# A blocked matmul with GELU: another home for one partial result, and another order for twelve loads

## Chip, cores, metric

One core of a Trainium2 chip. The time is that of one execution on the device in microseconds (us); lower is better. Unless a run says otherwise, times are medians of several executions. A profile is one further look at one execution, and its times are counted from that execution's first instruction.

## The reference

```python
m, k, n = 4096, 4096, 4096
a, b = randn(m, k), randn(k, n)           # float32
x = a @ b
out = 0.5 * x * (1 + tanh(sqrt(2 / pi) * (x + 0.044715 * x**3)))
```

## The kernel before

The kernel halves the matrices each way (A11, A12, ... B22) and computes blocks with seven products M1 to M7 instead of eight (a scheme of Strassen's kind), in 16-bit floats. There are 16 blocks. Block 0 must start before its data is there: the first half of its contraction (suffix _0) is done plainly, quadrant by quadrant, in 16 steps; the second half (suffix _1) with the seven products M3, M5, M7, M1, M4, M2, M6. A full product is 64 matmuls in four quarters; in block 0's second half only its last two quarters, 32 matmuls, are left. What the plain half gives for the output quarters is kept as partials C12 and C21 and added later.

TensorE accumulates in two chains of PSUM banks: X takes M5, M7, M1, M4 one on top of the other, Y takes M3, M2, M6. So a product may start on a bank only when the copy or result of the one before it has been read out. VectorE makes the sums of quadrants (aS, bS), transposes A (aT), and forms the results; ScalarE copies banks out (`keep`; such a copy is called a snapshot below) and does the GELU; GpSimd issues the loads.

```python
PRODUCTS = [                       # name, chain, sum of A, sum of B
    ("M3", "Y", "11", ("12", "22", 1)),
    ("M5", "X", ("11", "12", -1), "22"),
    ("M7", "X", ("12", "22", -1), ("21", "22", 1)),
    ("M1", "X", ("11", "22", -1), ("11", "22", -1)),
    ("M4", "X", "22", ("21", "11", 1)),
    ("M2", "Y", ("22", "21", -1), "11"),
    ("M6", "Y", ("21", "11", -1), ("11", "12", 1)),
]
# ... in plain(n): what becomes of a partial (i is one of RT = 4 row blocks)
            elif quad == "12":
                post[c, i] = keep("x7", acc, RT)
# ... in settle(gi, name, i), after the last matmul of a product on bank i
        if name == "M5":
            ...
                m5 = keep("m5", X, 2)
            y = new_y()                               # one of 5 output buffers
            tt(y, Y, m5, ALU.subtract)
            waiting.append((gi, i, 0, 1, y, y))
        elif name == "M7" and not end:
            post["x7", i] = keep("x7", X, RT)
        elif name == "M1":
            post["x1", i] = keep("x1", X, RT)
            later.append((gi, i))
        elif name == "M2":
            y = new_y()
            tt(y, post.pop(("x1", i)), Y, ALU.subtract)
            ...
        elif name == "M6":
            y = new_y()
            tt(y, Y, post.pop(("x7", i)), ALU.add)
            ...
# ... flush(): adds the partial of block 0 to a waiting result, then GELU and output
# ... the loads of block 0 by step: A, B load, T transpose; "+" weaves two loads evenly
        (8, "A11_1+B12_1+B22_1"),
        (9, "T22_0 A12_1+B21_1"),
        (14, "T11_1 A22_1 B11_1"),
        (16, "T12_1 A21_1"),
# ... the main loop
        for n, step in enumerate(steps):
            for fn, args in before.get(n, ()):        # loads and transposes
                fn(*args)
            if n + AHEAD < len(steps):                # AHEAD = 2
                gi, s, q = steps[n + AHEAD]
                if s >= 0:
                    make_sums(gi, s, q)
            if step[:2] != (0, 2):
                flush()
            combine()
            plain(n) if step[1] < 0 else multiply(*step)
            if step == (0, 2, QPH - 1):
                flush()
```

## Time and profile before

| | before |
|---|---|
| time, median of 3 | 1579.69 us (1579.39 to 1583.17) |
| span of the profiled execution | 1579.0 us |
| TensorE busy | 1566.6 us, 99% |
| VectorE busy over the whole span; in 74.2 to 122.4 us | 78%; 47.80 of 48.20 us |
| waits of TensorE in block 0's second half | 1.28, 0.38, 0.41, 1.80 and, entering the third quarter of block 1's M3, 0.28 us |

The kernel is bound by TensorE almost everywhere. The lines that carry this stand in the prediction. In rows in order of time, the first number is the start, the second the duration, and the bracket is the idle time of the engine before the row with what ended it.

### The profile page before, as it was taken

The numbers are of one execution on the slowest core, as the hardware profiler recorded it, in microseconds if no ns is written. First come the engines' busy times: TensorE is split into PE (matmuls) and PEld (weight loads), VectorE is DVE, ScalarE is ACT, GpSimd is POOL, SyncE is SP. The second block draws the span as 40 slices with busy tenths as digits, with TensorE's granted clock in tenths as the row PEclk, the third lists the DMA queues.
The fourth block names the chain that finished last, engine by engine and source line by source line (L and its number), as shares of the span: only waits on it lengthen the run. The fifth ranks groups of instructions, "written<-read, shape, count | busy, mean of one in ns | idle before, by whom it ended". The sixth has DMA issues, their size and how long they took to land. (4 is left out here: it accounts for less than half of the span.)

```text
span 1579.0 us, 19681 instructions
## 1 busy us (share of the span) xinstructions
PE 1566.6 (99%) x7246; PEld 709.1 (45%) x7246; DVE 1233.6 (78%) x1381; ACT 517.7 (33%) x710; POOL 537.6 (34%) x980
## 2 busy tenths in 40 slices
PE   9999999999999999999999999999999999999998
PEld 4444444444444444444444444444444444444443
DVE  1598888967787888895778788887687778988775
ACT  1026445311122545531111344542211145364111
POOL 7763442430234144341124413245011443314400
PEclk9999999999999999999999999999999999999999
DMA  9998784892957388586497837779468885748802
GB/s 179 197 223 175 123 171 74 159 168 43 197 104 153 92 133 160 107 174 120 83 162 117 186 72 141 148 112 186 77 121 146 134 160 94 149 105 134 160 28 82
DMA packets 225047, 211.13 MB, mean 134 GB/s; under 512 B 20144, under 2 KB 192176, under 8 KB 224944
## 3 DMA queue, kind: packets, MB, share of 16 engines
q0 software_dynamic: 187648, 142.67, 61.4%
q1 hardware_dynamic: 37296, 67.13, 11.8%
q8 instruction: 59, 0.97, 0.2%
q14 instruction: 44, 0.36, 0.1%
HBM read 285.22 MB, written 67.11 MB: 223 GB/s over the span
## 5 line engine op out<-in xcount | busy, mean ns | idle before, releaser
L331 PEld LDWEIGHTS <-aS 128*128 128x128 f16 x4960 | 485.3, 98 | 589.8 <-issue 2.8
L186 POOL DMA_DIRECT2D bR<-in_b_dram x832 | 447.6, 544 | 696.8 <-DVE bS L302 331.9
L302 DVE TENSOR_TENSOR aS<-aT 128x2048 f16<-128x2048 f16 (+1 forms) x312 | 376.3, 1212 | 150.2 <-PE accX L331 113.8
L331 PE MATMUL accX<-bS,aS 128*128 128x512 f16 x1984 | 431.5, 379 | 2.6 <-ACT x L395 1.8
L302 DVE TENSOR_TENSOR bS<-bR 128x2048 f16<-128x2048 f16 x310 | 376.2, 1218 | 69.0 <-PE accX L331 58.5
L331 PEld LDWEIGHTS <-aT 128*128 128x128 f16 x1984 | 194.1, 98 | 234.5 <-issue 0.6
L422 ACT ACTIVATE y<-y 128x512 f32<-128x512 f32 x192 | 118.2, 630 | 348.3 <-DVE y L431 348.2
L331 PE MATMUL accX<-bR,aS 128*128 128x512 f16 x992 | 216.7, 379 | 1.3 <-DVE aS L302 1.3
L331 PE MATMUL accY<-bS,aT 128*128 128x512 f16 x992 | 216.9, 379 | 0.3 <-DVE bS L302 0.3
L331 PE MATMUL accY<-bR,aS 128*128 128x512 f16 x992 | 216.7, 379 | 0.0
L331 PE MATMUL accX<-bS,aT 128*128 128x512 f16 x992 | 216.7, 379 | 0.0
L331 PE MATMUL accY<-bS,aS 128*128 128x512 f16 x992 | 216.7, 379 | 0.0
L186 POOL DMA_DIRECT2D stage<-in_a_dram x144 | 89.9, 631 | 252.7 <-DVE aT L161 178.7
L431 DVE TENSOR_TENSOR energy<-energy,square 128x1024 bf16<-128x1024 bf16 x240 | 164.5, 686 | 9.9 <-ACT square L207 5.7
L395 ACT COPY x<-accX 128x512 f32<-128x512 f32 x128 | 74.9, 585 | 227.1 <-PE accX L331 221.1
L207 ACT ACTIVATE square<-aT 128x1024 bf16<-128x1024 f16 x120 | 123.5, 1051 | 70.7 <-DVE energy L431 70.3
L207 ACT ACTIVATE square<-bR 128x1024 bf16<-128x1024 f16 x120 | 123.0, 1050 | 62.1 <-DVE energy L431 60.7
L161 DVE STREAM_TRANSPOSE aT<-stage 128x2048 uint32<-128x2048 uint32 (+1 forms) x37 | 74.6, 2018 | 48.1 <-DMA stage<-in_a_dram 42.0
L395 ACT COPY m<-accX 128x512 f32<-128x512 f32 x60 | 34.7, 579 | 219.5 <-PE accX L331 216.4
L422 ACT ACTIVATE y<-accX 128x512 f32<-128x512 f32 x64 | 38.2, 597 | 100.1 <-PE accX L331 99.9
L431 DVE TENSOR_TENSOR x<-accX,x 128x512 f32<-128x512 f32 x64 | 44.0, 691 | 21.8 <-ACT y L422 19.0
L431 DVE TENSOR_TENSOR y<-accY,m 128x512 f32<-128x512 f32 x60 | 39.9, 687 | 12.5 <-ACT m L395 12.4
(38 smaller groups left out, 343.0 us busy)
## 6 DMA issues: line engine op xcount, KB each, us to landing
bR<-in_b_dram POOLq DMA_DIRECT2D x832, 128.0 KB, 5.2
out_dram<-y SPq DMA_DIRECT2D x256, 256.0 KB, 5.6
stage<-in_a_dram POOLq DMA_DIRECT2D x112, 256.0 KB, 6.7
stage<-in_a_dram POOLq DMA_DIRECT2D x32, 128.0 KB, 5.1
row<-seen_d SPq DMA_DIRECT2D x2, 1.5 KB, 4.4
seen_d<-seen SPq DMA_DIRECT2D x1, 3.0 KB, 6.4
```

The lines of the kernel that those rows point to most:

```text
L161: nc.vector.transpose(dst[:, :, x, :], src[:, :, x, :])
L186: nc.gpsimd.dma_start(out=dst, in_=src)
L207: nc.scalar.activation(t[:, :], src, ACT.Square)
L302: nc.vector.tensor_tensor(out=x, in0=y, in1=z, op=ALU.add if o[2] > 0 else ALU.subtract)
L331: nc.tensor.matmul(acc[:, :], sa[:, j // 2, i * P : (i + 1) * P, j % 2], sb[:, j, :], start=start and j == 0, stop=stop and j == 3, skip_g ...
L395: nc.scalar.copy(out=t[:, :], in_=src[:, :])
L422: nc.scalar.activation(y[:, :], src[:, :], ACT.Gelu_apprx_tanh)
L431: nc.vector.tensor_tensor(out=o[:, :], in0=x[:, :], in1=y[:, :], op=op)
```

## The change

It aims at two of the waits. Partial C12 lay in the buffers of M7's snapshot, so the snapshot had to wait until C12 was added; it moves to those of M1's snapshot, which are needed one product later. And A12_1, for which M5 waits, is woven with only half of B21_1 (every second of its tiles, "a"), the other half ("b") following.

```diff
             elif quad == "12":
-                post[c, i] = keep("x7", acc, RT)
+                post[c, i] = keep("x1", acc, RT)
@@ the loads
-        (9, "T22_0 A12_1+B21_1"),
+        (9, "T22_0 A12_1+B21_1a B21_1b"),
@@ their reading: a suffix a or b picks a half
-                args = [(x[0], (0, x[1:3], int(x[4]), h)) for x in what.split("+")]
+                args = [
+                    (x[0], (0, x[1:3], int(x[4]), "ab".index(x[5]) if x[5:] else h))
+                    for x in what.split("+")
+                ]
```

## The prediction

> **What bounds the kernel now.** I read the page first, then the table of waits for TensorE, then the matmuls in order of time, then VectorE in order of time over the same stretch, and last the loads one by one.
>
> ```profile
> PE 1566.6 (99%) x7246; PEld 709.1 (45%) x7246; DVE 1233.6 (78%) x1381; ACT 517.7 (33%) x710; POOL 537.6 (34%) x980
> ...
> 129.70:1573.30 1443.60, 1443.60 (x6688) 654.34 (x6687) 1157.56 (x1293) 493.18 (x670) 445.29 (x811) 1.00 0.69 127
> 74.20:122.40 48.20, 44.34 (x204) 19.73 (x203) 47.80 (x55) 13.94 (x24) 33.31 (x61) 1.00 1.25 219
> ```
>
> The first line is the page's busy times; the other two are rows of the table by stretches (length, then busy time and count of PE, PEld, DVE, ACT, POOL, then granted clock, DMA share, GB/s). TensorE bounds the kernel: from 129.7 us to the end it is never idle. Nothing can be won there, and both parts of the change act earlier, in the first of the blocks. In 74.2 to 122.4 us it is VectorE that is full: 47.80 of 48.20 us.
>
> ```profile
> PE accX L331 <- ACT x L395: 1.8, 1, 1.8
> PE accX L331 <- DVE aS L302: 1.7, 2, 1.3
> ...
> 69.42 7.07 PE L331 MATMUL accY<-bS,aT 128*128 128x512 f16 x32
> 77.77 7.08 PE L331 MATMUL accX<-bR,aS 128*128 128x512 f16 x32 [1.28 <-DVE aS L302]
> 84.69 0.59 PE L331 MATMUL accX<-bS,aS 128*128 128x512 f16 x2
> 85.66 1.47 PE L331 MATMUL accX<-bS,aS 128*128 128x512 f16 x6 [0.38 <-DVE aS L302]
> 87.54 5.34 PE L331 MATMUL accX<-bS,aS 128*128 128x512 f16 x24 [0.41 <-ACT m L395]
> 94.68 7.07 PE L331 MATMUL accX<-bS,aS 128*128 128x512 f16 x32 [1.80 <-ACT x L395]
> 101.58 7.07 PE L331 MATMUL accX<-bS,aT 128*128 128x512 f16 x32
> ...
> 129.66 7.07 PE L331 MATMUL accY<-bS,aT 128*128 128x512 f16 x32 [0.28 <-DVE bS L302]
> ```
>
> The rows are the products of block 0's second half: M3 (69.42), M5 (77.77), M7 (84.69), M1 (94.68), M4, M2, M6, then M3 of block 1 at 122.30, whose third quarter starts at 129.66. An undisturbed product of 32 matmuls takes 101.58 - 94.68 = 6.90 us, 0.216 us each. From 69.42 to 129.66 there are 256 matmuls, 55.27 us, in 60.24 us: TensorE loses **4.97 us** here, in five places: about 1.44 before M5, 0.54 and 0.58 inside M7, 1.96 before M1, 0.45 at 129.66 (start to start, so a little more than the bracketed idle times). That is the ceiling for this change, 0.31% of the time.
>
> ```profile
> 69.62 0.69 DVE L431 TENSOR_TENSOR x<-x,accY 128x512 f32<-128x512 f32 x1 [0.67 <-PE accY L362]
> 74.14 2.31 DVE L161 STREAM_TRANSPOSE aT<-stage 128x2048 uint32<-128x2048 uint32 x1 [3.83 <-DMA stage<-in_a_dram]
> 76.49 2.36 DVE L302 TENSOR_TENSOR aS<-aT 128x2048 f16<-128x2048 f16 x2
> ...
> 93.27 2.49 DVE L431 TENSOR_TENSOR y<-y,x 128x512 f32<-128x512 f32 x4
> ...
> 118.16 2.50 DVE L431 TENSOR_TENSOR y<-y,c 128x512 f32<-128x512 f32 x4
> ...
> 125.05 0.69 DVE L431 TENSOR_TENSOR y<-accY,x 128x512 f32<-128x512 f32 x1 [2.66 <-DMA out_dram<-y]
> ...
> 128.39 1.22 DVE L302 TENSOR_TENSOR bS<-bR 128x2048 f16<-128x2048 f16 x1
> ```
>
> VectorE stands idle for 3.83 us until the last piece of A12_1 lands, turns it (74.14), makes M5's aS (76.49; M5 has waited for it), and then runs in order without a gap of note to 122.4. The row at 93.27 adds partial C12 to M5's results. ScalarE's copy of M7 goes into the same four buffers, so it waits for this row, and M1, which accumulates in M7's bank, waits for the copy: the 1.80 us. The row at 128.39 is the sum that M3 of block 1 waits for at 129.66. So the wait at 129.66 is the end of a VectorE chain that began at 74.14.
>
> **What the Trainium skill says.** "TensorE: Matmul & The Clock Gate", back-to-back issue gap: 512 columns at full clock, some 216 ns apart; the trace has 216 ns (6.90 us / 32), so a product cannot go faster. "VectorE: DVE Perf Modes", the perf-mode tier table and the errata section: a 16-bit tensor_tensor of 2048 elements 1224 ns, an fp32 one of 512 elements 691 ns; the trace has 1.22 us and 0.69 us, so these rows do not shrink. "Perfetto Trace Analysis", Tensor Engine Instruction: Vector and Scalar engines are strict FIFO; the trace agrees (the row at 93.27 stands behind M1's sums at 88.73 to 93.3 though its operands were older). "DMA: Bandwidth & Descriptors", issuing engines are not separate DMA queues: all DMAs share 16 engines and interleave; here the 12 loads concerned land in the order of issue, at 196 to 200 GB/s over that stretch.
>
> **Part 1, the C12 buffers.** No instruction is added or taken away: ScalarE's four copies, VectorE's adds are the same rows with other buffers. Removed: M7's copies no longer wait for the row at 93.27; the build of the changed kernel shows them waiting for TensorE alone. M7's first bank is then copied in 0.28 + 0.59 us after its last matmul, some 2.6 us before M7 ends, so M1 starts unhindered. Added: M1's copies must wait for C12's add. M1's first bank ends at about 90.3 + 4.3 = 94.6 us by then, the add ends before 93.5: no wait. By itself this pulls TensorE forward by 1.96 us at M1, but VectorE's rows do not move, so M3 of block 1 still waits for the row at 128.39. **Worth alone: about 0.**
>
> **Part 2, the loads.** The 12 loads are 4 of A12_1 (256 KB) and 8 of B21_1 (128 KB), 16 units of 128 KB. They land from 64.3 (58.74 + 5.6) to 74.7 us (67.32 + 7.4), issue time plus time to landing read row by row; the load before ends at about 63.65, so a unit takes (74.7 - 63.65) / 16 = 0.69 us. The order was b A b b A b b A b b A b: the fourth A is behind 15 units and lands at 66.67 + 7.4 = 74.07. The changed kernel issues A b A b A b A b b b b b: 11 units, 63.65 + 7.6 = 71.25, that is **2.8 us earlier**. VectorE is free from 70.3, so the transpose starts at 71.35 instead of 74.14. The last B21_1 piece still lands at 74.7 and is needed at 78.8 - 2.8 = 76.0. A22_1's second half lands at 74.97 + 5.1 = 80.1, is needed at 83.64 - 2.8 = 80.8: near, but in time.
>
> Now the sum, both parts together. VectorE, dense from the transpose on, runs 2.8 us earlier throughout. M5 starts at 76.33 (loss gone), M7 at 83.2 (its sums are ready at 82.1 and 82.8), M1 at 90.2, M4 97.1, M2 104.0, M6 110.9, M3 of block 1 at 117.8, its third quarter could start at 124.7. The sum it needs is ready at 129.6 - 2.8 = 126.8: a wait of **about 2.1 us**, in place of 0.3. Before that row VectorE waits for an output buffer: 118.16 + 0.69, gelu 0.63, landing some 5.5 us later, 125.05; all of it is set off by VectorE, so it moves by 2.8 as well if the landing takes as long. So TensorE recovers about 4.97 - 2.1 = 2.8 us: VectorE's shift, not the sum of the waits. From there on TensorE is dense, and the end moves by as much: 1579.69 - 2.8 = 1576.9; I say **1577.0**.
>
> **Rivals.** (a) The waits add up: all five go and nothing replaces them, -5.0 us, 1574.7. For it: 1.96 + 1.44 are named by the table of waits, and the two parts of the change aim exactly at them. Against it: VectorE's 47.80 of 48.20 us; for 5 us its chain would have to start before A12_1 can land. (b) The A12 pieces land no earlier, or A22_1 or B21_1 become the new wait, because the DMA engines are full either way: then VectorE's start moves by under 1 us and the time is 1579 to 1579.7. For it: only 0.7 us of reserve at A22_1, and POOL lets only eight loads be open at a time. Against it: the order within a full queue is exactly what the change alters, and the queue lands in order. (c) The output landing at 125.05 does not move along, because it competes with the loads of block 1 (landings there take 5.3 to 7.6 us, loads up to 9.7): it could eat 1 us or give 1: 1576 to 1578.
>
> **Range and chances.** The chain reading with a shift of 2.8 +- 0.8 us has some 7 in 10, (b) 1 in 10, between the two readings and towards (a) the rest. Runs of the kernel before spread from 1579.39 to 1583.17, so a median may be off by half a us: 1575.4 to 1579.0. 2% would be 31.6 us, six times the ceiling, and nothing that is added could cost as much: faster 0.005, within 2% 0.99, slower 0.005.
>
> **What would show it.** Right: the transpose at about 71.3; M5 at 76.4 with no wait; no wait of M1 for ScalarE; VectorE still without gaps to about 119.6; a wait for bS of about 2 us at the third quarter of block 1's M3, which starts near 126.9; nothing after. Wrong: if that wait stays below 0.5 us and the gain is over 4 us, VectorE was no bound; if VectorE waits for A22_1 at 80, rival (b); if the transpose comes early and the row after 125 does not, rival (c).

## The result, and the profile after

The changed kernel took 1578.82 us (1577.87 to 1579.90, 6 runs), the kernel before, of the same rounds, 1580.76 us (1579.39 to 1583.17, 6 runs). The ratio of the times is 0.9988, interval 0.9975 to 1.0001. That is 1.9 us less, inside the range, but less than the 2.8 us forecast; and no difference that the interval alone proves.

First view: the waits of TensorE in the changed kernel (total, times, longest, in us).

```profile
PE accY L331 <- DVE y L431: 1.8, 1, 1.8
PE accX L343 <- DVE table L583: 1.4, 1, 1.4
PE accY L331 <- DVE bS L302: 0.5, 1, 0.5
PE accY L362 <- DMA bR<-in_b_dram: 0.5, 1, 0.5
```

Both waits that the change aimed at are gone. The first line is new, and the prediction did not have it. Second view: TensorE's rows in order of time, from M3 in block 0 on.

```profile
70.27 7.07 PE L331 MATMUL accY<-bS,aT 128*128 128x512 f16 x32
77.18 7.07 PE L331 MATMUL accX<-bR,aS 128*128 128x512 f16 x32
84.08 14.05 PE L331 MATMUL accX<-bS,aS 128*128 128x512 f16 x64
97.97 7.07 PE L331 MATMUL accX<-bS,aT 128*128 128x512 f16 x32
104.88 7.07 PE L331 MATMUL accY<-bR,aS 128*128 128x512 f16 x32
113.72 7.07 PE L331 MATMUL accY<-bS,aS 128*128 128x512 f16 x32 [1.77 <-DVE y L431]
120.62 7.07 PE L331 MATMUL accY<-bS,aT 128*128 128x512 f16 x32
128.23 7.07 PE L331 MATMUL accY<-bS,aT 128*128 128x512 f16 x32 [0.54 <-DVE bS L302]
```

M3 to M2 run through without a wait. Then M6 (113.72) stands 1.77 us, and the third quarter of block 1's M3 (128.23) 0.54 us. Third view: VectorE's rows in order of time that the argument needs.

```profile
72.09 2.31 DVE L161 STREAM_TRANSPOSE aT<-stage 128x2048 uint32<-128x2048 uint32 x1 [0.93 <-DMA stage<-in_a_dram]
...
81.99 1.25 DVE L161 STREAM_TRANSPOSE aT<-stage 128x1024 uint32<-128x1024 uint32 x1 [0.44 <-DMA stage<-in_a_dram]
...
112.99 2.48 DVE L431 TENSOR_TENSOR y<-x,accY 128x512 f32<-128x512 f32 x4
...
116.51 2.49 DVE L431 TENSOR_TENSOR y<-y,c 128x512 f32<-128x512 f32 x4
...
123.45 0.69 DVE L431 TENSOR_TENSOR y<-accY,x 128x512 f32<-128x512 f32 x1 [2.71 <-DMA out_dram<-y]
```

The row at 112.99 is what M6 waits for: M2's results, read out of the Y banks on which M6 accumulates. They could be formed from about 109 us on (M2's first bank is full 20 matmuls after 104.88), but the four rows of sums for M6 stand ahead of them on VectorE.

The start-up is not the change's doing, but it moves the numbers. M3 starts at 70.27 us here and at 69.42 before. The 46 warm-up matmuls on zeros ended later here (the plain part started at 14.37 against 13.07 us), a difference that a later wait for a load (0.49 instead of 0.94 us) took partly back. A repeat of the same kernel (`after_again`, below) started M3 at 69.32 us, a repeat of the kernel before at 69.55. So three measures are used, each a difference between starts of rows; the first two leave the start-up out:

- **load lead**: VectorE's transpose of A11_1 to its transpose of A12_1. Small is early.
- **chain**: the transpose of A12_1 to the third quarter of block 1's M3 on TensorE. Where that row is merged with the half before it, 6.905 us (32 matmuls) are added to M3's start.
- **stretch**: block 0's M3 to that third quarter. It also holds how far the loads are behind TensorE: stretch = load lead + chain - the time from A11_1's transpose to M3, which was 6.81 us before and after, but between 5.33 and 6.81 us in the 14 profiles.

| | load lead | chain | stretch |
|---|---|---|---|
| before | 11.53 | 55.52 | 60.24 |
| after | 8.63 | 56.14 | 57.96 |

The stretch fell by 2.28 us; 0.85 us of it is missing from the span because of the later start, and the output at the very end landed about 0.5 us sooner: 1579.0 - 2.28 + 0.85 - 0.5 = 1577.1, the span measured. The load lead fell by 2.9 (2.8 forecast). The chain grew by 0.62, where the forecast had it constant.

### The profile page after: what moved, and what is told of

The parts are those of the page before. It is cut to its first block, busy times and chain, and to the rows that moved or that the text cites. A ratio compares the mean times of both kernels' runs of the same rounds, so it can differ in the third digit from the quotient of the medians.

```text
span 1577.1 us, 19678 instructions
## 1 busy us (share of the span) xinstructions
PE 1567.7 (99%) x7246; PEld 709.6 (45%) x7246; DVE 1233.7 (78%) x1381; ACT 518.0 (33%) x710; POOL 537.7 (34%) x980
```

## The experiments

Twelve runs. **Theory D** (the prediction's): VectorE, filled in order from the transpose of A12_1 on, sets the end of the stretch, so a wait removed downstream comes back as another. **Theory A**: each removed wait is a gain of its own.

### Each part alone, and both kernels again

The edits: `c12_only` has only the first hunk of the diff, `loads_only` only the others; `after_again` and `before_again` are the two kernels unchanged.

> Part 1 alone (C12 in M1's buffers, loads as before). Measure: the stretch from the first matmul of M3 in block 0 to the third quarter of M3 in block 1, 60.24 us before and 57.96 us after, which leaves out the start-up. Theory D (VectorE's dense chain sets the stretch): the 1.80 us before M1 goes, a wait of about 1.8 us before M6 for VectorE's y rows appears, stretch 60.2 +- 0.3, time ratio 1.000. Theory A (waits add up): stretch 58.3, time lower by 1.9 us, ratio 0.9988.

> Part 2 alone (loads woven anew, C12 in M7's buffers). Theory D: VectorE's rows move by as much as with the whole change; M1 still waits about 1.9 us for ScalarE, but the wait before M6 is gone, so stretch 58.0 +- 0.4, ratio to before 0.9985 and to the changed kernel 1.000. Theory A: M5's wait and those in M7 go, the one before M1 stays: stretch about 58.2 too, but then the two parts together would have to reach 56.3, which the changed kernel did not.

> The changed kernel again. Theory D: stretch 57.9 +- 0.4, a wait near 1.8 us before M6 and near 0.5 us before the third quarter of block 1's M3. If the wait of VectorE for the second half of A22_1 (0.44 us) is systematic it comes again; if it was chance it is absent in one of the runs with the new loads and the stretch is then 57.5. Time ratio 0.9988 +- 0.0008.

> The kernel before again, for the spread. Stretch 60.2 +- 0.3 as the program is the same. The start of M3 (69.42 us before, 70.27 after, programs identical up to there) is expected to differ by up to 1 us from run to run with the time at which the full clock is granted; if all runs of one program have the same start, that explanation is wrong. Time ratio 1.000.

| run | load lead | chain | stretch | time, median (5 runs) | ratio to before (interval) |
|---|---|---|---|---|---|
| c12_only | 11.11 | 56.10 | 61.56 | 1580.86 | 1.0004 (0.9990 to 1.0017) |
| loads_only | 8.65 | 55.45 | 58.35 | 1577.78 | 0.9985 (0.9972 to 0.9999) |
| after_again | 9.13 | 56.49 | 59.69 | 1579.63 | 0.9993 (0.9980 to 1.0007) |
| before_again | 11.11 | 55.44 | 60.01 | 1580.06 | 1.0002 (0.9988 to 1.0016) |

The kernel before of these rounds: 1580.07 us.

On the start that `before_again` asked about: from 4 to 8 us 21 warm-up matmuls ran in `before`, 13 in `after` and in `before_again`, 15 in `after_again`, so the pace at the start differs between executions of one program; the granted clock reads 1.00 in all four, so no column shows why.

C12 alone gained nothing, as theory D had it (A: 1.9 us). The new loads alone gave all that the change gave, though M1's wait for ScalarE was there in full. The rows of TensorE in `loads_only`, M1 and M6 and the third quarter:

```profile
95.45 7.07 PE L331 MATMUL accX<-bS,aS 128*128 128x512 f16 x32 [1.79 <-ACT x L395]
...
116.16 7.07 PE L331 MATMUL accY<-bS,aS 128*128 128x512 f16 x32
...
130.36 7.07 PE L331 MATMUL accY<-bS,aT 128*128 128x512 f16 x32 [0.22 <-DVE bS L302]
```

M1 waits 1.79 us and M6 not at all; in the changed kernel it is the other way round, 0 and 1.77 us. The wait moved from M1 to M6. It could, because both waits hang on VectorE's chain and end at nearly the same time: in `loads_only` M1 starts 20.54 us after the transpose of A12_1, which puts M6 three products later, at 41.25; in `after_again` M6 starts at 41.24, after VectorE's row for M2. That the two agree so closely is a property of this program; it makes each of them worth nothing alone. (`loads_only` started late in its profile: a wait of 2.32 us for a load in the plain part put M3 at 72.01 us. One of its five timed runs was 1581.64 us, the others 1577.70 to 1578.42.)

Two things were not expected. `after_again` gained only 0.4 us by medians, and its stretch of 59.69 us misses the 57.9 +- 0.4 expected. Against `after` that is 1.73 us more: 0.50 in the load lead, 0.35 in the chain (56.49 us, the longest of these, with a wait of 1.28 us at the third quarter), and 0.88 because the loads were further behind TensorE (A11_1's transpose 5.93 instead of 6.81 us before M3). So it looked as if C12's new place lengthened the chain, 56.1 to 56.5 in three profiles against 55.4 to 55.5 in three. And `c12_only`'s stretch was longer than before's, though theory D said equal. Table by stretches for `c12_only` (length, busy time and count of PE, PEld, DVE, ACT, POOL, granted clock, DMA share, GB/s):

```profile
77.00:79.00 2.00, 0.11 (x1) 0.12 (x2) 1.97 (x3) 0.00 (x0) 1.60 (x4) 1.00 1.44 193
79.00:81.00 2.00, 2.00 (x7) 0.83 (x7) 2.00 (x2) 0.00 (x0) 1.59 (x4) 0.64 1.38 197
81.00:83.00 2.00, 2.00 (x7) 0.67 (x5) 2.00 (x3) 0.00 (x0) 1.51 (x3) 0.51 1.24 205
```

Here A12_1 landed late, M5 waited 2.02 us, and for some 4 us after it the clock was granted at 0.51 to 0.64: M5 took 8.60 us from start to start instead of 6.91. This spell added 1.7 us to M5. The stretch of 61.56 us is therefore no measure of C12; of the excess in its chain, 0.21 us arose while VectorE worked through the same rows (40.71 us from the transpose to M2's first result, 40.50 in `before`).

### Does the chain run through the output buffers?

In the profiles with the longer chain, VectorE's waits at M6's results for an output buffer to land were longer or later. The rows in `after_again` (the kernel before has 118.16 and 125.05, shown in the prediction):

```profile
116.55 2.49 DVE L431 TENSOR_TENSOR y<-y,c 128x512 f32<-128x512 f32 x4
...
124.16 0.69 DVE L431 TENSOR_TENSOR y<-accY,x 128x512 f32<-128x512 f32 x1 [3.38 <-DMA out_dram<-y]
```

Such a result can do without an output buffer: M6 adds M7's snapshot, which is dead afterwards.

```diff
         elif name == "M6":
-            y = new_y()
-            tt(y, Y, post.pop(("x7", i)), ALU.add)
+            x7 = post.pop(("x7", i))
+            y = new_y() if gi else x7
+            tt(y, Y, x7, ALU.add)
```

`after_inplace` is the changed kernel with this edit, `loads_inplace` is `loads_only` with it. A second edit, `after_order`, takes away the wait before M6 by placing M6's second pair of sums behind M2's results; `after_both` has both edits.

```diff
+            late = step == (0, 5, QPH - 1)
-            if n + AHEAD < len(steps):
+            if n + AHEAD < len(steps) and not late:
                 ...
                 multiply(*step)
+            if late:
+                make_sums(*steps[n + AHEAD])
```

> The changed kernel, with M6 of block 0 written into M7's snapshot buffers, so that these four results need no output buffer and wait for no output landing. Measure, free of the start-up: from the start of VectorE's transpose of the late A12_1 to the third quarter of M3 in block 1; so far 55.4 to 55.5 us in three runs with C12 in M7's buffers and 56.1 to 56.5 us in three with C12 in M1's. Theory O (C12's new place costs 0.7 to 1.0 us because M2's outputs land later and hold VectorE at M6's rows): VectorE's waits for outputs go, no wait at that third quarter, the wait of about 1.8 us before M6 stays, measure 55.0 to 55.4. Theory P (the cost is the wait before M6 itself): measure stays at 56.1 or more. Time to before: O 0.9980, P 0.9990.

> The new loads alone (C12 in M7's buffers) with M6 of block 0 in M7's snapshot buffers. Theory O: only the 0.4 us lost at the third quarter goes, measure 55.0 to 55.1, equal to that of the changed kernel in place, so that the place of C12 costs nothing any more: time 0.9980 of before, within 0.3 us of the other. Theory P: this one is 0.7 us or more faster than the changed kernel in place.

> The changed kernel, M6's second pair of sums in block 0 placed behind M2's four result rows on VectorE instead of ahead of them; output buffers as they were. It takes away the wait before M6 (1.77 us) and nothing else. If the chain over VectorE, output and VectorE sets the end of the stretch, the wait comes back at the third quarter of block 1's M3, about 2.3 to 3 us long, and the measure stays at 56.1 to 56.5, the time at 0.999. If the wait before M6 is what counts, the measure falls by 1.8 to 54.5.

> Both: M6 in place and the sums behind the results. Nothing is left that holds TensorE between M1 and block 1, if VectorE was bound by order and by outputs and not by its amount of work: measure 53.6 to 54.0, waits before M6 and at the third quarter under 0.4 us, time lower by 2 us than the changed kernel and by 4 us than before, 0.9972. If VectorE's amount of work is the bound, the measure stays above 54.8.

| run | load lead | chain | stretch | time, median | ratio to before (interval) |
|---|---|---|---|---|---|
| after_inplace | 8.54 | 55.08 | 56.84 | 1577.85 (5 runs) | 0.9985 (0.9971 to 0.9998) |
| loads_inplace | 8.63 | 55.06 | 57.39 | 1577.88 (5 runs) | 0.9985 (0.9971 to 0.9998) |
| after_order | 8.84 | 54.84 | 58.35 | 1578.70 (6 runs) | 0.9997 (0.9984 to 1.0009) |
| after_both | 8.54 | 53.52 | 55.25 | 1575.87 (5 runs) | 0.9975 (0.9961 to 0.9988) |

The kernel before of these rounds: 1580.09 us.

With M6 in place the chain is 55.08 and 55.06 us, whichever buffers C12 is in, and no third quarter waits (M6's wait of 1.43 us holds the one, M1's of 1.80 us the other). So the excess lay in the way from M2's results over the output landing to VectorE's next rows, as theory O had it, and not in the wait before M6 (P). Whether C12's place makes outputs land later is a further question, and stays open. The time ratios, 0.9985 twice, do not separate O (0.9980) from P (0.9990). In `after_inplace` M6 still waits:

```profile
112.45 7.07 PE L331 MATMUL accY<-bS,aS 128*128 128x512 f16 x32 [1.43 <-DVE y L431]
119.36 13.98 PE L331 MATMUL accY<-bS,aT 128*128 128x512 f16 x64
```

`after_order` fell between the two forecasts: M6's wait went and 1.29 us came back at the third quarter, so most of the gain was eaten, but the chain of 54.84 us is shorter than the 56.1 expected:

```profile
127.75 7.07 PE L331 MATMUL accY<-bS,aT 128*128 128x512 f16 x32 [1.29 <-DVE bS L302]
```

The outputs landed faster in that profile: from the row that adds C21 to the first M6 result that needs a buffer it took 6.11 us, where `after` took 6.94 and `after_again` 7.61. (The profile puts this row's wait down to TensorE, which had long been done with that bank, so it was read as an output's.) Its timed runs scatter (1578.14 to 1582.18 us), and the ratio of 0.9997 shows no gain.

`after_both` has neither wait; TensorE from M6 on:

```profile
111.19 7.07 PE L331 MATMUL accY<-bS,aS 128*128 128x512 f16 x32
118.10 13.98 PE L331 MATMUL accY<-bS,aT 128*128 128x512 f16 x64
```

Its stretch is 55.25 us for 256 matmuls, 55.24 us at 6.905 us for 32: TensorE loses nothing any more. It is correct, and the fastest of all: 4.2 us under the kernel before by medians, with an interval clear of 1.

### What is C12's place worth then, and does VectorE's work count?

`loads_both` is `after_both` with C12 back in M7's buffers. The extra runs make VectorE form M4's sums of block 0 twice, with the same result: `after_extra` from the changed kernel, `both_extra` from the fastest. `c12_again` repeats `c12_only`.

```diff
-                nc.vector.tensor_tensor(
-                    out=x, in0=y, in1=z, op=ALU.add if o[2] > 0 else ALU.subtract
-                )
+                for _ in range(2 if (gi, s) == (0, 4) else 1):
+                    nc.vector.tensor_tensor(
+                        out=x, in0=y, in1=z, op=ALU.add if o[2] > 0 else ALU.subtract
+                    )
```

> The fastest version so far (M6 in place, sums behind results), but with C12 back in M7's buffers. Asks what the C12 part is worth once nothing else holds TensorE. If waits replace each other, M1 waits some 1.8 us for ScalarE again, nothing after it waits, and the measure (late A12_1 transpose to third quarter) is 55.1 against 53.5 with C12 in M1's buffers: the part that cost 0.7 us or nothing by itself is then worth 1.6 us. If C12's place never matters, 53.5. Time 1.0010 of the fastest version, 0.9985 of before.

> The changed kernel with VectorE doing both sums for M4 of block 0 twice (same result), 2 rows of 1.13 us more in the full stretch. If VectorE's chain sets the end of the stretch, all of it is paid: measure 58.4 to 58.8 instead of 56.1 to 56.5, time +2.3 us on the changed kernel, the wait before M6 near 4 us. If it is hidden, measure and time stay.

> The fastest version with the same two extra rows. M2's first result there is ready about 0.7 us before M6 starts, so 2.27 us more on VectorE should cost some 1.5 us: measure 55.0 (53.5 without), a wait of about 1.4 us before M6. If VectorE's order and not its load were all that matters, 53.5.

> Part 1 alone once more, because its first profile had a spell of half clock in M5. Theory: measure 55.5 to 56.5 (55.44 for the kernel before), a wait of 1.4 to 1.8 us before M6 and over 0.5 us at the third quarter, none before M1; time 1.0000 to 1.0006 of before. Spell of half clock absent, unless M5's wait reaches 2 us again.

| run | load lead | chain | stretch | time, median (5 runs) | ratio to before (interval) |
|---|---|---|---|---|---|
| loads_both | 9.15 | 55.06 | 57.41 | 1577.81 | 0.9983 (0.9969 to 0.9997) |
| after_extra | 8.50 | 60.03 | 61.95 | 1582.51 | 1.0009 (0.9996 to 1.0023) |
| both_extra | 9.00 | 55.88 | 58.09 | 1578.33 | 0.9991 (0.9977 to 1.0004) |
| c12_again | 11.12 | 55.39 | 59.73 | 1580.55 | 0.9999 (0.9985 to 1.0013) |

The kernel before of these rounds: 1580.63 us.

`loads_both` came out as forecast: M1 waits 1.79 us for ScalarE, nothing after it waits, and the chain is 55.06 against 53.52. The same hunk that is worth nothing alone is worth 1.5 us of the chain once the two other holds are gone (by the ratios to before, 0.9983 against 0.9975, some 1.3 us, with intervals that overlap).

The extra work was paid. Each extra row took 1.25 us of VectorE instead of the 1.13 supposed, 2.5 together. In `after_extra` M6 starts 43.75 us after the transpose, 2.5 later than the 41.24 of `after_again`:

```profile
115.50 9.53 PE L332 MATMUL accY<-bS,aS 128*128 128x512 f16 x32 [3.90 <-DVE y L432]
```

But the wait was then 3.9 us long, and the clock was granted at 0.50 to 0.62 from 115 to 121 us: M6's 32 matmuls took 9.37 us from start to start, 2.5 us too long. That accounts for the chain of 60.03: 55.06 (no output wait is left for TensorE) + 2.5 + 2.5. In `both_extra` (its line numbers are one higher) the forecast was 55.0, the chain 55.88: beside the wait before M6 there is one inside it, for the sums that now stand behind M2's results, and of the 2.5 us the chain pays 2.36:

```profile
113.12 3.61 PE L332 MATMUL accY<-bS,aS 128*128 128x512 f16 x16 [1.63 <-DVE y L432]
117.18 3.61 PE L332 MATMUL accY<-bS,aS 128*128 128x512 f16 x16 [0.45 <-DVE bS L303]
```

`c12_again` shows that C12 in M1's buffers need not lengthen the chain: it is 55.39 us, as short as before's and just under the 55.5 to 56.5 expected, and the third quarter waits 0.18 us where over 0.5 was expected. Its time ratio is 0.9999. In TensorE's rows the wait is again at M6, none at M1:

```profile
87.74 12.25 PE L331 MATMUL accX<-bS,aS 128*128 128x512 f16 x56 [0.41 <-ACT m L395]
...
115.57 7.07 PE L331 MATMUL accY<-bS,aS 128*128 128x512 f16 x32 [1.77 <-DVE y L431]
```

## Why the prediction was right, and where not

**The direction and the mechanism hold; the time was hit with some luck.** The 1578.82 us lie 0.2 us inside the range, and the repeat, 1579.63, lies outside it, with 0.4 us gained in place of 2.8. The mechanism is better shown than the number: the gain is VectorE's shift and not the sum of the waits. Part 1 alone was put at about 0: ratios 1.0004 and 0.9999. Part 2 was to carry the gain: 0.9985 alone, beside 0.9988 and 0.9993 for the whole change (intervals of about 0.13% either way). Rival (a), 1574.7, did not come; its 5 us needed two more edits, and then came nearly (4.2 us).

**The term for the loads was a little too large.** Four units of 0.69 us gave 2.8. The load lead was 11.53, 11.11, 11.11 and 11.12 us in the four profiles with the old order (mean 11.22) and 8.50 to 9.15 in ten with the new one (mean 8.76): 2.46 us. The profile of `after` alone, against that of before, shows 2.9.

**The step that failed is "VectorE, dense from the transpose on, runs 2.8 us earlier throughout".** It treated the chain as of fixed length. It was 55.39 to 55.52 us in four profiles (`before` twice, `loads_only`, `c12_again`), but 56.14 and 56.49 in the two of the changed kernel, and 56.10 in `c12_only` with its spell of low clock. In `after`, 0.40 is A22_1's second half landing late, the narrow reserve of rival (b): VectorE waits 0.44 us at 81.99, which it does in one of the ten profiles with the new loads. The rest is the output landing of rival (c). From the row adding C21 to the first M6 result that waits for a buffer it took 7.61 us in `after_again`, against 6.89, 6.81 and 6.81 in the three profiles with C12 in M7's buffers; in `after` it took 6.94, and from there to the last M6 result 2.91 against 2.73 us, so 0.2 to 0.3 in all. The remedy shows that this way is it (55.08 and 55.06 in place). So 2.46 for the loads less 0.6 to 1.0 for the chain make 1.5 to 1.9 us. The two timed comparisons gave 1.9 and 0.4 by medians; the second falls short by what the prediction did not count, the loads further behind TensorE (0.88 us in its profile).

**The new wait was put in the wrong place.** About 2.1 us were expected at the third quarter of block 1's M3. They came as 1.77 before M6 and 0.54 (1.28 in `after_again`) there. I had asked of M6 only whether its sums were ready, not whether M2's results had left the banks that it writes. For the end of the stretch it made little difference, as both hang on the same order of rows on VectorE. It did for the remedy: one edit for each was needed.

**"VectorE is full" was right for the wrong reason in one respect.** Extra rows cost nearly their full time in the chain (2.36 of 2.5 us in `both_extra`), so it is the bound as soon as anything is added. But moving two of its rows and freeing four others from output buffers let TensorE run without a gap with the same amount of VectorE work. It was the order of the rows as much as their sum.

**On a citation.** The section from which the prediction takes 216 ns also puts matmuls of 512 columns in a sustained stream at some 131 ns. Nothing here comes near that: 6688 matmuls in 1443.60 us are 216 ns each. That a product cannot go faster is a reading of this trace, not of the page.

**Open.** Whether outputs land later with C12 in M1's buffers, or whether that was chance, is not settled: with that layout and M6 in output buffers the way took 7.07 (`c12_only`), 6.94 and 7.61 us, but 6.77 in `c12_again`; with rows moved or added as well, 6.11 (`after_order`) and 8.09 (`after_extra`). M4's GELU rows begin 30.4 us after the transpose with it and 32.0 us without (`after`, `before`), so their stores are issued 1.6 us earlier among the loads of block 1, yet no run isolates that. What sets the start of M3 (69.32 to 72.01 us) and the lag of the loads behind it is not shown either. The intervals of the timings (about 0.13% either way) do not separate the changed kernel from `loads_only`.

## What to carry to other kernels

When one wait on the bounding engine is removed, ask who supplies the next thing it needs: if the same engine in strict order supplies both, the wait only moves, and the gain is how much earlier that engine's chain starts. Look at every condition of each later start, the operands and also the bank or buffer that must be free. A part that is worth nothing alone can be worth its full wait once the other links of the chain are loosened, so judge the parts together.

## What the Trainium skill lacked or had wrong

- **"TensorE: Matmul & The Clock Gate", the table under why this matters for your kernels**: it asks for no idle gaps above some 3 us between bursts. Here a gap of 2.02 us was followed by some 4 us at a granted clock of 0.51 to 0.64 (32 matmuls in 8.60 instead of 6.91 us), a gap of 2.32 us in another run by none, one of 3.9 us by a spell with 32 matmuls in 9.37 us. So a gap below the page's figure was followed by 1.7 us of lost time, and a longer one was not; what decides is not shown here.
- **"DMA: Bandwidth & Descriptors", issuing engines are not separate DMA queues**: right that stores and loads interleave, but it has no figure for how much a store's landing then varies among loads. Here the way from VectorE's row over GELU and a 256 KB store to the next use of the buffer took 6.11 to 8.09 us in five profiles with the same order of loads, and cost the chain up to 1.0 us (`after_again`).
